# Modulation vectors of a diffusion trunk: thirteen as row sums from one ordered list, three as products

## The chip, the cores and the metric

The kernel runs on one core of one Trainium2 chip. The metric is the device time of one execution in microseconds (us). The engines in the rows are PE (TensorE, matmuls; PEld is its weight load), DVE (VectorE), ACT (ScalarE), POOL (GpSimd) and SP (SyncE, which issues the weight loads). Each works through its own instructions in order and waits on semaphores for the others.

## What is computed

Two layers run over 128 context tokens and 128 latent tokens with the same weights. What matters here is the modulation: for each layer nine vectors of 1024, for two conditions (the context's learned vector and the latent's), enter the norms as shift and scale and the residuals as gate.

```python
def adaln(cvec, w, b):
    m = jax.nn.silu(cvec) @ w + b
    return jnp.split(m, N_MOD, axis=-1)

def trunk_layer(x, mods, lp, lam_init, ctx):
    sh1, sc1, gt1, sh2, sc2, gt2, sh3, sc3, gt3 = mods
    g = lp['g_norm']
    u = modulate(rms_norm(x, g[0]), sh1, sc1)
    x = x + 0.5 * gt1[:, None, :] * swiglu(u, lp['w_ffn1_in'], lp['w_ffn1_out'])
    u = modulate(rms_norm(x, g[1]), sh2, sc2)
    y, ctx_out = token_mixer(u, lp, lam_init, ctx)
    x = x + gt2[:, None, :] * y
    u = modulate(rms_norm(x, g[2]), sh3, sc3)
    x = x + 0.5 * gt3[:, None, :] * swiglu(u, lp['w_ffn2_in'], lp['w_ffn2_out'])
    return x, ctx_out
```

The mixer computes one projection W_in of u (z), three branches from it (differential attention, a Fourier mix, a bidirectional mLSTM), their merge with sigmoid gates, and W_out.

## The kernel before

The residual `xT` stays on chip, channels on partitions, in eight blocks of 128 x 256 (128 context and 128 latent columns). Every large product is computed in two parts for precision: a weight unit of up to 128 x 1024 is split into `whi` (ScalarE, L1484) and `wlo` (VectorE, L1485), and `mm3` issues three matmuls per block (L166 to L168). A unit of eight blocks is thus 24 matmuls of TensorE.

The program is a list of steps that `add` builds and the loop at the end runs through once, in Python, so the list's order is the order of the instructions on each engine. A step needs its units; after its own function the loop calls `pump_split`, which splits coming units while fewer than six (`N_SPLIT`) are live, and then the functions in `late`. Weights come in chunks of mostly 1 MB through six buffers (`N_RAW`), loaded by SP in the order of their first need; a chunk's buffer is given to the next one when its last unit is used.

A layer has an FFN (gate and value part of eleven pairs, four units each; output part of 24 units), the mixer (W_in, then for each of three branches its gates and its product, merged into `mg`, then the output projection of eight blocks) and a second FFN. The branches' own work runs in `lanes`, generators advanced by the mixer's steps. `residual` adds a block with its gate to `xT` and puts the next norm's work on that block into `late`: square and sum (ScalarE, GpSimd), the scaled block `y` and its two parts `yh`, `yl`. The last two blocks' part is `held` and done inside `first`, the step that starts the next part: it computes products on the unnormalised `y` while `stats`, `root` (`var`, then `rstd` on GpSimd), `diag` (`dg`) and `spread` (a broadcast by TensorE) make the norm's factor, and `apply` then writes the normalised `uh`, `ul`. The last steps ahead of `first` are marked so that they pump no splits.

A modulation vector is made in one of two ways. A product (`side` in `mod_steps`) multiplies the raw weights with both conditions on TensorE in four column groups, in two steps of eight matmuls, each two passes; a closing step transposes the sums, and `finish` adds the bias. A row sum reads the transposed weights `w_adaT`, 128 rows of 1024 to an instruction, multiplies them by a condition that lies on all partitions (`cb`) and accumulates, on VectorE: 16 such steps and a `finish` give a vector. Vectors 0 and 1 of layer 0 are made in `begin`. Of the other sixteen, `ADA` lists seven as row sums and nine as products, each in a part of the program, and `spread_into` puts the steps of a part at equal distances into it.

Of the kernel before, what the change touches and what calls it, by code (L numbers as in the profile page):

```python
# [119 lines left out]


@with_exitstack
def trunk_kernel(ctx: ExitStack, tc: tile.TileContext, a: dict):
# [94 lines left out]
    run = {"lanes": False}  # L218
# [77 lines left out]

    def mod_steps(mods_):
# [20 lines left out]
        def finish(l, m, o, x):  # L318
            bT = parT[l][:, m * KD:(m + 1) * KD].unsqueeze(2).to_broadcast([P, KD, 2])
            ve.tensor_add(o, x, bT)  # L320
            if m % 3 == 1:
                k0 = 72 + m // 3 * KD
                gT = parT[l][:, k0:k0 + KD].unsqueeze(2).to_broadcast([P, KD, 2])
                ve.scalar_tensor_tensor(o, o, 1.0, gT, op0=ALU.add, op1=ALU.mult)
            elif m % 3 == 2 and m != 5:
                ve.tensor_scalar(o, o, 0.5, None, op0=ALU.mult)

        for i, (l, m) in enumerate(on_ve):
            o, junk = mods[l, m], []
            for j in range(KD // 2):  # L330
                ch = Chunk(a["w_adaT"][l, m, j], 2, D)
                for b in range(2):
                    for g in range(2):
                        u = Unit(ch, b, b + 1, 0, D, split=False)

                        def fn(u=u, k=2 * j + b, g=g, o=o, l=l, m=m, junk=junk):
                            if not junk:
                                junk.append(blk([P, D], "junkw"))
# [1215 lines left out]
```

## Time and profile before

| | |
|---|---|
| median of 3 runs (lowest, highest) | 1361.5 us (1358.19, 1361.8) |
| profiled execution, its own time | 1359.85 us |
| its span, first to last instruction | 1358.1 us |
| mean granted TensorE clock | 0.99 of full |
| busy: PE, DVE, ACT, POOL | 98%, 71%, 50%, 8% of the span |
| read from HBM | 298.85 MB |

A busy row counts the time in which an engine has at least one instruction running; matmuls overlap, so busy tells nothing of how well each is used. Times in the rows are from the span's start. In a row of the timeline the first number is the start, the second the length, and a bracket at the end gives the idle time just before it and who ended that.

### The profile page before, as it was taken

Reading aid. Unit: us, or ns where it says so; the run is one execution under the profiler, and the core shown is the slowest. Engines: PE = TensorE matmul, PEld = TensorE weight load, DVE = VectorE, ACT = ScalarE, POOL = GpSimd, SP = SyncE. Lnnn points to the kernel's source line nnn. Section 1 sums busy time; section 2 is a strip of 40 time slices with the busy share of each in tenths; the row PEclk is TensorE's granted clock in tenths of the full one; section 3 lists DMA queues with packets and bytes.
Section 4 is the critical chain, followed back from the end, with each engine's and each line's share of the span. In section 5 each row is a group of like instructions: output and inputs, shape, how many; then the busy total and the mean of one; then the engine's idle time right before and its main releaser. Section 6 shows DMA issues by size and latency. Waiting matters only on the chain.

```text
span 1358.1 us, 25895 instructions
## 1 busy us (share of the span) xinstructions
PE 1328.9 (98%) x10752; PEld 1258.0 (93%) x10752; DVE 959.8 (71%) x1533; ACT 683.0 (50%) x1096; POOL 113.4 (8%) x137
## 2 busy tenths in 40 slices
PE   6999999999999999999999999999999999999998
PEld 3899999888998998999999999988899899999998
DVE  4589865786557589977669977677565668886653
ACT  4554444665544465444455444456554445744442
POOL 3000001300000030000020000130000001200001
PEclk8999999999999999999999999999999999999999
DMA  9999966563578846987538987648445895477630
GB/s 301 325 318 324 309 213 192 173 201 125 170 250 295 266 152 215 337 306 235 181 124 296 303 304 229 203 132 232 134 155 194 292 307 186 145 259 228 223 108 32
DMA packets 239990, 304.73 MB, mean 224 GB/s; under 512 B 5552, under 2 KB 212672, under 8 KB 236160
## 3 DMA queue, kind: packets, MB, share of 16 engines
q1 hardware_dynamic: 238048, 296.98, 66.8%
q0 software_dynamic: 1824, 6.10, 1.3%
q8 instruction: 84, 1.38, 0.4%
q14 instruction: 34, 0.28, 0.1%
HBM read 298.85 MB, written 3.15 MB: 222 GB/s over the span
## 4 chain that ended last, share of the span: by engine, by line
PE 84%; DVE 8%; DMA 3%; ACT 2%; issue 1%; SPq 0%; POOL 0%; DVEq 0%; ACTq 0%
PE pm L166 25%; PE pm L167 24%; PE pm L168 24%; PE pd L163 3%; DVE wlo L1485 3%; PE pb L163 2%; DMA raw<-w_ada 2%; DVE v L488 2%; ACT whi L1484 1%; DVE ul L178 1%; PE pm L742 1%; PE pm L743 1%; PE pm L744 1%; PE pa L163 1%; DVE junkw L339 1%
## 5 line engine op out<-in xcount | busy, mean ns | idle before, releaser
L1485 DVE TENSOR_TENSOR wlo<-raw,whi 128x1024 fp32r<-128x1024 f32 (+1 forms) x424 | 507.8, 1204 | 271.2 <-ACT whi L1484 263.6
L1484 ACT CAST whi<-raw 128x1024 fp32r<-128x1024 f32 (+1 forms) x424 | 433.5, 1032 | 337.2 <-PE pm L167 247.1
L166 PE MATMUL pm<-uh,whi 128*128 128x256 f32 x1928 | 551.3, 286 | 0.0
L168 PE MATMUL pm<-uh,wlo 128*128 128x256 f32 x1928 | 541.9, 281 | 4.8 <-DVE wlo L1485 4.8
L167 PE MATMUL pm<-ul,whi 128*128 128x256 f32 x1928 | 544.5, 282 | 1.7 <-DVE v L488 1.2
L166 PEld LDWEIGHTS pm<-uh,whi 128*128 128x128 f32 x1928 | 364.4, 189 | 15.8 <-ACT whi L1484 7.7
L168 PEld LDWEIGHTS pm<-uh,wlo 128*128 128x128 f32 x1928 | 364.3, 189 | 6.1 <-DVE wlo L1485 6.1
L167 PEld LDWEIGHTS pm<-ul,whi 128*128 128x128 f32 x1928 | 364.0, 189 | 3.8 <-DVE v L488 1.7
L167 PE MATMUL pm<-hl,whi 128*128 128x256 f32 x704 | 198.0, 281 | 0.0
L166 PE MATMUL pm<-hh,whi 128*128 128x256 f32 x704 | 197.6, 281 | 0.0
L168 PE MATMUL pm<-hh,wlo 128*128 128x256 f32 x704 | 197.5, 280 | 0.0
L339 DVE CUSTOM_DVE_ANT_0 junkw<-raw,cb 128x1024 f32<-128x1024 f32 x112 | 136.5, 1219 | 0.1
L168 PEld LDWEIGHTS pm<-hh,wlo 128*128 128x128 f32 x704 | 132.7, 189 | 0.0
L166 PEld LDWEIGHTS pm<-hh,whi 128*128 128x128 f32 x704 | 132.7, 189 | 0.0
L167 PEld LDWEIGHTS pm<-hl,whi 128*128 128x128 f32 x704 | 132.7, 188 | 0.0
L413 POOL TENSOR_TENSOR nsum<-nsum,nsq 128x256 f32<-128x256 f32 x36 | 36.5, 1013 | 814.8 <-ACT nsq L411 814.8
L163 PE MATMUL pd<-raw,cT 128*32 128x512 f32 (+1 forms) x416 | 46.0, 559 | 11.4 <-DMA raw<-w_ada 9.6
L643 ACT ACTIVATE silu<-pm 128x512 f32<-128x512 f32 x39 | 23.3, 596 | 55.0 <-PE pm L168 55.0
L177 ACT CAST hh<-silu 128x512 fp32r<-128x512 f32 (+1 forms) x42 | 25.5, 609 | 32.7 <-DVE silu L645 32.7
L558 DVE SCALAR_TENSOR_TENSOR xT<-pm,mod,xT 128x128 f32<-128x128 f32 x96 | 28.8, 342 | 18.1 <-PE pm L168 18.0
L1228 ACT ACTIVATE sig<-pm 128x512 f32<-128x512 f32 x24 | 14.3, 598 | 50.2 <-PE pm L168 50.1
L742 PE MATMUL pm<-whi,uh 128*128 128x512 f32 x96 | 39.3, 409 | 0.0
(339 smaller groups left out, 1726.1 us busy)
## 6 DMA issues: line engine op xcount, KB each, us to landing
raw<-w_ffn_in SPq DMA_DIRECT2D x88, 1024.0 KB, 6.9
raw<-w_ada SPq DMA_DIRECT2D x36, 1024.0 KB, 5.2
raw<-w_ffn_out SPq DMA_DIRECT2D x32, 1024.0 KB, 5.6
raw<-w_in SPq DMA_DIRECT2D x32, 1024.0 KB, 5.8
raw<-w_adaT SPq DMA_DIRECT2D x28, 1024.0 KB, 6.7
raw<-w_branch_gate SPq DMA_DIRECT2D x24, 1024.0 KB, 5.2
raw<-w_ffn_out SPq DMA_DIRECT2D x16, 768.0 KB, 4.6
raw<-w_ada SPq DMA_DIRECT2D x16, 512.0 KB, 7.1
```

The costliest lines, as they stand in the source:

```text
L163: pe.matmul(out, lhsT, rhs, start=start, stop=stop)
L166: pe.matmul(out, sh, mh, start=start, stop=False)
L167: pe.matmul(out, sh, ml, start=False, stop=False)
L168: pe.matmul(out, sl, mh, start=False, stop=stop)
L177: ac.copy(hi, src)
L339: ve.tensor_tensor_reduce(junk[0], u.raw()[:, 0, :], cb[:, g, :], 1.0, 0.0, op0=ALU.mult, op1=ALU.add, accum_out=o[:, k, g:g + 1])
L413: eng.tensor_add(self.sum, self.sum, sq)
L488: ve.tensor_scalar(v[:, G[1]], v[:, G[1]], self.scale[:, k, 1:2], self.shift[:, k, 1:2], op0=ALU.mult, op1=ALU.add)
L558: ve.scalar_tensor_tensor(xT[:, k, G[g]], ps[:, G[g]], gate[:, k, g:g + 1], xT[:, k, G[g]], op0=ALU.mult, op1=ALU.add)
L742: pe.matmul(ps[g], xh[:, G[g]], wh, start=(k == 0), stop=False)
L1484: ac.copy(u.hi, r)
L1485: ve.tensor_sub(u.lo, r, u.hi.bitcast(F32))
```

## The change

`ADA` keeps three products: layer 0's vector 2 in its first FFN, and vector 5 of each mixer. The other thirteen stand in `ROWS`, in the order in which they are made; `row_steps` yields their 208 steps. Every step of the program carries a rate: 0.85 in the gate and value part of an FFN, 0.7 in its output part, 0.3 in W_in and the first two branches, 0.9 from the third branch on to the mixer's end; zero in the start of the program. When the sum of the rates passes one, the next row step is put behind that step. The list lasts from layer 0's first FFN to the third branch of layer 1. `finish` moves out of `mod_steps` unchanged, the target of the products that a row sum throws away becomes one fixed bf16 tile, `residual` asserts that its vectors are made, and `s_params2` (lambdas, masks) moves up by two pairs.

```diff
-CT = 8
-
-ADA = {(0, "ffn1"): ([(0, 4), (0, 3)], [(0, 2)]),
-       (0, "mixer"): ([], [(0, 7), (0, 6), (0, 5)]),
-       (0, "ffn2"): ([(1, 1), (1, 0)], [(0, 8)]),
-       (1, "ffn1"): ([(1, 4), (1, 3)], [(1, 2)]),
-       (1, "mixer"): ([], [(1, 7), (1, 6), (1, 5)]),
-       (1, "ffn2"): ([(1, 8)], [])}
+CT = 0
+
+ADA = {(0, "ffn1"): [(0, 2)], (0, "mixer"): [(0, 5)], (1, "mixer"): [(1, 5)]}
+ROWS = [(0, 4), (0, 3), (0, 7), (0, 6), (1, 1), (1, 0), (0, 8), (1, 2), (1, 4), (1, 3), (1, 7), (1, 6), (1, 8)]
+
+RATE = {"in": 0.85, "out": 0.7, "win": 0.3, "branch": 0.3, "merge": 0.9}
...
+    junkw = const.tile([P, D], BF16, name="junkw")
...
     def add(fn, units=(), pump=True, ln=False, ahead=()):
         steps.append(Step(fn, units, pump, ln, ahead))
+        steps[-1].rate = run["rate"]
...
+    def row_steps():
+
+        for l, m in ROWS:
+            o = mods[l, m]
+            for j in range(KD // 2):
+                ch = Chunk(a["w_adaT"][l, m, j], 2, D)
+                for b in range(2):
+                    for g in range(2):
+                        u = Unit(ch, b, b + 1, 0, D, split=False)
+
+                        def fn(u=u, k=2 * j + b, g=g, o=o, l=l, m=m):
+                            ve.tensor_tensor_reduce(junkw, u.raw()[:, 0, :], cb[:, g, :], 1.0, 0.0,
+                                                    op0=ALU.mult, op1=ALU.add, accum_out=o[:, k, g:g + 1])
+                            if k == KD - 1 and g == 1:
+                                finish(l, m, o, o)
+                                known.add((l, m))
+
+                        yield fn, [u]
...
+        run["rate"] = 0.0 if begun else RATE["in"]
         for jj in range(n_pair):
-            if jj == 4 and l == 0 and which == 1:
+            if jj == 2 and l == 0 and which == 1:
                 add(s_params2)
+                run["rate"] = RATE["in"]
...
         p1 = len(steps)
+        run["rate"] = RATE["out"]
...
+        run["rate"] = RATE["win"]
         add(lambda: first(norm, us, q_done), us, pump=2)
...
         p0 = len(steps) + 6
+        run["rate"] = RATE["branch"]
...
+                    if bi == 2:
+                        run["rate"] = RATE["merge"]
                     add(drain)
...
+    todo, due = row_steps(), 0.0
+    for s in steps:
+        s.slot = []
+        due += s.rate
+        while due >= 1.0:
+            due -= 1.0
+            nxt = next(todo, None)
+            if nxt is not None:
+                s.slot.append(Step(*nxt))
+    steps[:] = [x for s in steps for x in (s, *s.slot)]
+    assert next(todo, None) is None
```

A row step is an ordinary step, so it also pumps splits. The order of instructions shows what this makes of three places.

First, TensorE where layer 0's mixer comes to the branch of the attention. `uh`, `ul` are the normalised input that the gates use, `ah` the attention's output; `raw` with `cT` is a product. Before:

```order
L166 MATMUL pm<-uh_2787,whi 128x256
L167 MATMUL pm<-ul_2789,whi 128x256
L168 MATMUL pm<-uh_2787,wlo 128x256
L163 MATMUL pd<-raw_4358,cT 32x512 x4
L163 MATMUL pd<-raw_4437,cT 32x512 x4
L166 MATMUL pm<-ah,whi 128x256
```

After:

```order
L165 MATMUL pm<-uh_2813,whi 128x256
L166 MATMUL pm<-ul_2815,whi 128x256
L167 MATMUL pm<-uh_2813,wlo 128x256
L165 MATMUL pm<-ah,whi 128x256
L166 MATMUL pm<-al,whi 128x256
```

The product's matmuls between the gates and the branch are gone; in the whole program 6 such pieces remain of 18.

Second, VectorE at the end of layer 0's merge. `sig` is a branch's product times its gate, `mg` the merged sum and `mgl` its second part, `xT` the residual's update by the first two blocks of the output projection. Before:

```order
L1256 TENSOR_TENSOR sig<-sig,pm 128x512
L1257 TENSOR_TENSOR mg_4390<-mg_4390,sig 128x512
L178 TENSOR_TENSOR mgl_5319<-mg_4390,mgh_5318 128x512
L1256 TENSOR_TENSOR sig<-sig,pm 128x512
L1257 TENSOR_TENSOR mg_4390<-mg_4390,sig 128x512
L178 TENSOR_TENSOR mgl_5319<-mg_4390,mgh_5318 128x512
L1485 TENSOR_TENSOR wlo<-raw_5070,whi 128x1024 x2
L558 SCALAR_TENSOR_TENSOR xT<-pm,mod_5_101,xT 128x128 x4
```

After (the two rows with `junkw` and without are one row sum):

```order
L1267 TENSOR_TENSOR sig<-sig,pm 128x512
L1268 TENSOR_TENSOR mg_4417<-mg_4417,sig 128x512
L177 TENSOR_TENSOR mgl_5327<-mg_4417,mgh_5326 128x512
L319 ISA junkw,mod_1_106<-raw_4955,cb 128x1024
L319 ISA mod_1_106 128x1
L1509 TENSOR_TENSOR wlo<-raw_5087,whi 128x1024
L1267 TENSOR_TENSOR sig<-sig,pm 128x512
L1268 TENSOR_TENSOR mg_4417<-mg_4417,sig 128x512
L177 TENSOR_TENSOR mgl_5327<-mg_4417,mgh_5326 128x512
L1509 TENSOR_TENSOR wlo<-raw_5087,whi 128x1024
L319 ISA junkw,mod_1_106<-raw_5167,cb 128x1024
L319 ISA mod_1_106 128x1
```

A row sum and a split now stand between the last two blocks of the merge, and the second split and another row sum ahead of `xT`.

Third, VectorE at the end of the same output projection, where the second FFN's norm begins with `var`. Before:

```order
L558 SCALAR_TENSOR_TENSOR xT<-pm,mod_5_101,xT 128x128 x2
L1485 TENSOR_TENSOR wlo<-raw_5151,whi 128x1024
L426 TENSOR_SCALAR y<-xT,mod_7_103 128x128
L178 TENSOR_TENSOR yl_5431<-y,yh_5429 128x256
L558 SCALAR_TENSOR_TENSOR xT<-pm,mod_5_101,xT 128x128 x4
L463 TENSOR_SCALAR var<-pb 128x2
```

After:

```order
L559 SCALAR_TENSOR_TENSOR xT<-pm,mod_5_101,xT 128x128 x2
L1509 TENSOR_TENSOR wlo<-raw_5297,whi 128x1024
L426 TENSOR_SCALAR y<-xT,mod_7_103 128x128
L177 TENSOR_TENSOR yl_5443<-y,yh_5441 128x256
L559 SCALAR_TENSOR_TENSOR xT<-pm,mod_5_101,xT 128x128 x2
L319 ISA junkw,mod_1_106<-raw_5332,cb 128x1024
L319 ISA mod_1_106 128x1
L1509 TENSOR_TENSOR wlo<-raw_5371,whi 128x1024
L559 SCALAR_TENSOR_TENSOR xT<-pm,mod_5_101,xT 128x128 x2
L319 ISA junkw,mod_1_106<-raw_5332,cb 128x1024
L319 ISA mod_1_106 128x1
L1509 TENSOR_TENSOR wlo<-raw_5371,whi 128x1024
```

`var` comes next there: behind each of the last two blocks stand a row sum and a split. The same pattern stands at the end of both first FFNs, and at the end of layer 0's second FFN one row sum with two splits.

## Rows read from the trace of the kernel before

**Rows 1.** The page, busy us (share of the span) xinstructions of each engine:

```profile
PE 1328.9 (98%) x10752; PEld 1258.0 (93%) x10752; DVE 959.8 (71%) x1533; ACT 683.0 (50%) x1096; POOL 113.4 (8%) x137
```

**Rows 2.** Busy time by stretch: stretch, us, busy by engine, clock, DMA share, GB/s:

```profile
0.00:55.00 55.00, 41.09 (x308) 27.99 (x309) 22.66 (x56) 21.01 (x40) 11.81 (x20) 0.84 1.05 305
55.00:1340.00 1285.00, 1274.92 (x10346) 1217.70 (x10345) 933.78 (x1469) 659.82 (x1053) 100.15 (x115) 1.00 0.68 223
1340.00:1358.00 18.00, 12.94 (x103) 12.35 (x101) 3.41 (x9) 2.21 (x4) 1.48 (x2) 0.84 0.16 59
```

**Rows 3.** Chain that ended last, pieces of products: start, us, what:

```profile
382.63 1.85 PE pd L163 x16
...
1083.46 1.85 PE pd L163 x16
```

**Rows 4.** Timeline of PE, transposes of a closing step:

```profile
1122.07 0.60 PE L171 MATMUL pd<-cst,adaev 128*128 128x128 f32 x4
```

**Rows 5.** PE's waits for a product's weights, 500 to 560 and 720 to 760 us:

```profile
PE pd L163 <- DMA raw<-w_ada: 0.8, 1, 0.8
...
PE pd L163 <- DMA raw<-w_ada: 0.7, 1, 0.7
```

**Rows 6.** Timeline of DVE in layer 0's first FFN, a row sum and a split:

```profile
105.76 1.22 DVE L339 CUSTOM_DVE_ANT_0 junkw<-raw,cb 128x1024 f32<-128x1024 f32 x1
...
106.91 1.22 DVE L1485 TENSOR_TENSOR wlo<-raw,whi 128x1024 fp32r<-128x1024 f32 x1
```

**Rows 7.** That FFN's gate and value part by stretch; DVE's timeline in its output part:

```profile
100.00:165.00 65.00, 65.00 (x550) 63.43 (x549) 60.20 (x84) 30.17 (x36) 0.00 (x0) 1.00 0.96 330
...
176.83 1.23 DVE L1485 TENSOR_TENSOR wlo<-raw,whi 128x1024 fp32r<-128x1024 f32 x1 [1.61 <-ACT whi L1484]
179.67 1.23 DVE L1485 TENSOR_TENSOR wlo<-raw,whi 128x1024 fp32r<-128x1024 f32 x1 [1.61 <-ACT whi L1484]
```

**Rows 8.** Busy time by stretch, end of layer 0's mixer:

```profile
476.00:500.00 24.00, 24.00 (x205) 24.00 (x205) 21.73 (x43) 14.77 (x28) 6.87 (x6) 1.00 0.52 177
```

**Rows 9.** Timeline of DVE in layer 0's output projection:

```profile
492.66 0.59 DVE L558 SCALAR_TENSOR_TENSOR xT<-pm,mod,xT 128x128 f32<-128x128 f32 x2
...
494.31 0.76 DVE L426 TENSOR_SCALAR y<-xT,mod 128x128 f32<-128x128 f32 x1
...
495.33 0.60 DVE L558 SCALAR_TENSOR_TENSOR xT<-pm,mod,xT 128x128 f32<-128x128 f32 x2
```

**Rows 10.** End of layer 0's merge: timeline of PE and of DVE:

```profile
476.05 0.28 PE L166 MATMUL pm<-mgh,whi 128*128 128x256 f32 x1
...
478.35 0.69 DVE L178 TENSOR_TENSOR mgl<-mg,mgh 128x512 fp32r<-128x512 f32 x1 [0.69 <-ACT mgh L177]
```

**Rows 11.** Timeline of DVE, last update and the norm's start:

```profile
498.91 0.61 DVE L558 SCALAR_TENSOR_TENSOR xT<-pm,mod,xT 128x128 f32<-128x128 f32 x2 [0.32 <-PE pm L168]
501.13 0.16 DVE L463 TENSOR_SCALAR var<-pb 128x2 f32<-128x2 f32 x1 [1.62 <-PE pb L163]
501.21 0.28 DVE L426 TENSOR_SCALAR y<-xT,mod 128x128 f32<-128x128 f32 x1
```

**Rows 12.** Timeline of DVE, from layer 0's first FFN to the mixer:

```profile
232.51 0.61 DVE L558 SCALAR_TENSOR_TENSOR xT<-pm,mod,xT 128x128 f32<-128x128 f32 x2 [1.52 <-PE pm L168]
234.74 0.16 DVE L463 TENSOR_SCALAR var<-pb 128x2 f32<-128x2 f32 x1 [1.61 <-PE pb L163]
```

**Rows 13.** PE's waits in the attention, 286 to 296 and 946 to 956 us:

```profile
PE pa L171 <- DVE pc L855: 1.1, 1, 1.1
...
PE pa L171 <- DVE pc L855: 1.4, 1, 1.4
```

**Rows 14.** Busy time by stretch, clock after a stall:

```profile
34.00:36.00 2.00, 1.65 (x16) 0.68 (x16) 0.13 (x1) 0.00 (x0) 0.00 (x0) 0.50 0.91 239
...
952.00:954.00 2.00, 2.00 (x15) 2.00 (x14) 1.63 (x4) 1.96 (x6) 1.08 (x2) 0.69 0.05 6
```

**Rows 15.** Busy time by stretch, most of layer 0's branches:

```profile
340.00:470.00 130.00, 130.00 (x1091) 119.51 (x1090) 79.11 (x132) 59.90 (x101) 4.64 (x5) 1.00 0.74 249
```

More of the change, by code (lines that the diff above doesn't have):

```diff
@@ L119, in __init__ @@
         self.ahead = list(ahead)
+        self.rate = 0.0
 @with_exitstack
@@ L217, in trunk_kernel @@
     lanes = [[], [], []]
-    run = {"lanes": False}
+    run = {"lanes": False, "rate": 0.0}
     late, held = [], []
@@ L316, in side @@
                 ac.copy(st["ev"], st["ps"])
[L318 to L338, printed above, removed]
-                            ve.tensor_tensor_reduce(junk[0], u.raw()[:, 0, :], cb[:, g, :], 1.0, 0.0,
-                                                    op0=ALU.mult, op1=ALU.add, accum_out=o[:, k, g:g + 1])
-                            if k == KD - 1 and g == 1:
-                                finish(l, m, o, o)
-                        seq.append(((i + (4 * j + 2 * b + g) / 16) / len(on_ve), fn, [u]))
         for i, (l, m) in enumerate(mods_):
@@ L356, in fn @@
                               for e in range(2) for c in range(2)], 0, 512)
-                seq.append(((2 * i + j2 + 0.4) / (2 * len(mods_)), fn, us))
-        seq.sort(key=lambda x: x[0])
-        out = [x[1:] for x in seq]
-        if not mods_:
-            return out
+                out.append((fn, us))
         def post():
@@ L378, in post @@
                 finish(l, m, mods[l, m], full[:, :, 2 * i:2 * i + 2])
+                known.add((l, m))
         out.append((post, []))
@@ L554, in prod8, with residual @@
                 mid()
-    def residual(k, ps, gate, norm):
+    def residual(k, ps, gate, norm, of):
+        assert of <= known, (of, known)
         for g in range(2):
@@ L585, in add_ffn @@
         gate = mods[l, 2 if which == 1 else 8]
+        of = {(l, 2), (l, 3), (l, 4)} if which == 1 else {(l, 8), (l + 1, 0), (l + 1, 1)}
+        of = {x for x in of if x[0] < DEPTH}
         hT = {}
@@ L1268, in mk_ @@
             return mg["h", k // 4][:, k % 4, :], mg["l", k // 4][:, k % 4, :]
-        gate = mods[l, 5]
+        gate, of = mods[l, 5], {(l, 5), (l, 6), (l, 7)}
         for mp in range(4):
@@ L1288, in fn @@
                     prod8(p_, u, mk_)
-                    residual(m, p_, gate, norm_next)
+                    residual(m, p_, gate, norm_next, of)
                 add(fn, [us_[i]], pump=mp < 3)
-        spread_into(p0, len(steps) - 8, mods_)
+        if mods_:
+            spread_into(p0, len(steps) - 8, mods_)
         return loads
@@ L1414, in trunk_kernel @@
     for l in range(DEPTH):
-        add_ffn(l, 1, norms[l, 0], norms[l, 1], ADA[l, "ffn1"], begin if l == 0 else None)
+        add_ffn(l, 1, norms[l, 0], norms[l, 1], ADA.get((l, "ffn1")), begin if l == 0 else None)
         pos = len(steps)
-        steps.insert(pos - 6, Step(add_mixer(l, norms[l, 1], norms[l, 2], ADA[l, "mixer"]), pump=False))
-        add_ffn(l, 2, norms[l, 2], norms[l + 1, 0], ADA[l, "ffn2"])
+        steps.insert(pos - 6, Step(add_mixer(l, norms[l, 1], norms[l, 2], ADA.get((l, "mixer"))), pump=False))
+        add_ffn(l, 2, norms[l, 2], norms[l + 1, 0], ADA.get((l, "ffn2")))
     def fin():
```

20 lines of the change are left out of this document (15 added, 5 removed).

## The prediction

> **What bounds the kernel now.** I read the busy line first. TensorE is busy 98% of the span, VectorE 71% [rows 1]. Then where TensorE is idle: of 29.1 us, 19.0 lie in the first 55 us and the last 18 us, which the change leaves nearly as they are, and 10.1 are spread over the 1285 us between [rows 2]. So a microsecond of TensorE work taken out of the middle is a microsecond gained, as long as VectorE, which takes the work over, keeps up everywhere. Its share is an average, and I look for stages in which it has no room. The sum is made against the profiled execution, 1359.85 us around a span of 1358.1; it lies 1.65 us under the median of the three runs, 1361.5, within their spread of 3.6.
>
> **Products removed.** A modulation product is two pieces of 16 TensorE passes, and a piece holds the in-order TensorE for 1.85 us [rows 3], which show the first and the last of those that go; of 18 pieces 12 go, four in each mixer and two each in layer 0's second FFN and layer 1's first. 12 x 1.85 = 22.2 us. Of five closing steps two go, each with four transposes, 0.60 us [rows 4]: 1.2 us. In those two FFNs a product also waited for its weights, 0.8 and 0.7 us [rows 5]: 1.5 us, gone with it. Gain: 24.9 us, all on the path that sets the end.
>
> **Rows added.** 208 row sums stand in place of 112, so 96 more. In a full queue one takes VectorE 1.14 us (from the row at 105.76 to the split at 106.91, the accumulator read hidden) [rows 6]: 110 us. Most of it is hidden. With a row at nearly every step layer 0's first FFN ran VectorE at 93% while TensorE was busy throughout [rows 7], so the rate of 0.85 in the other gate and value parts, about what two of them have now, costs nothing. In the output parts a split comes every 2.84 us, takes 1.23 and leaves 1.61 idle before the next [rows 7]: a row at 0.7 a step fits. Layer 1's second FFN loses its rows. The DMA volume does not change. The bf16 target of the row I cost at nothing; it is written by the same stream. The lambda steps, two pairs earlier in layer 0's first FFN, bring their two table loads and small operations with them; they stay under the splits done ahead.
>
> **Where it does not fit: the end of layer 0's mixer.** In the output projection VectorE repeats update, split, two scalings in one group and difference in 2.67 us (from xT at 492.66 to xT at 495.33) [rows 9], and TensorE's step is 2.84: no room. From 476 to 500 us VectorE is busy 21.7 of 24 us [rows 8]. The new order puts seven row sums between the last merge block but one and the last xT, and one split ahead of it that used to come after: 8 x 1.14 = 9.1 us. Of the 2.3 us idle some 0.5 can take a row; the rest are waits inside a chain (sig, mg, the ScalarE cast, mgl) that remain. So the last xT ends 8.6 us later. Behind it one row and one split (2.3 us) stand ahead of var, where 1.62 us were idle [rows 11]: 0.7 more. var starts the norm's chain, for which TensorE waits at its next broadcast, and PSUM buffers that xT frees are late too, so TensorE cannot run ahead. **9.2 us.** Bounds: 10 instructions x 1.14 less all idle time, 11.4 - 3.9 = 7.5, to 11.4.
>
> **Three other norms.** Row steps now stand between the last block of an FFN and the next norm, where no step pumped splits before, and each also lets a split go ahead. For both mixers two rows and two splits come ahead of var (4.6 us) where 1.5 and 1.6 us were idle [rows 12]; with the wait for ScalarE's cast I get var 2.0 us later. Some 0.7 comes back, as those splits are not to be done after the norm: 1.3 each. From layer 0 to layer 1 it is one row and two splits, 3.4 less 1.6, of which 0.4 comes back: 1.4. Sum **4.0 us**, bounds 0 and 7.
>
> **Layer 1's merge.** One row and one split stand ahead of the last sig, and VectorE comes there 0.5 to 1 us late: the last mgl, ready at 478.35 + 0.69 in layer 0's copy of the place, comes 2.8 us later. TensorE starts on mgh at 476.05 [rows 10] and needs the last block after 36 matmuls of 0.12 us, at 480.4, so 1.3 us are slack: **1.5 us** (0 to 2.8). In layer 0 the same wait is inside the 9.2.
>
> **Attention in the mixers.** TensorE waits 1.1 and 1.4 us for pc [rows 13]. At 0.3 rows a step one or two rows fall into the full stretch ahead of it: 1.5 + 1.1 = **2.6 us** (0 to 5, four rows, since earlier ones fall into VectorE's wait for the swapped queries). Nothing of SP's queue is new there but row chunks in place of weight columns; the swap is issued behind a load that waits for a split on VectorE, as now.
>
> **Clock.** At 950 to 954 us a stall of 1.4 us is followed by a granted clock of 0.69 of 2.4 GHz, and after the wait for weights near the start the clock was 0.50, its 1.2 GHz level, for 34 to 36 us [rows 14]. Longer stalls now stand at five places: I take **2 us** (0 to 6). The Trainium skill (TensorE: Matmul & The Clock Gate, part 1, The HAM clock gate) calls the half rate the default and activity what releases it; the rows agree, and by it each stall is paid again in slow matmuls, the second rival.
>
> **A rule against the rows.** Where VectorE's scaling y runs beside GpSimd's sums in the output projection it takes 0.76 us, and 0.28 when alone [rows 9, 11]. The Trainium skill (SBUF — State Buffer, Summary: rules for kernel authors) says that a VectorE instruction with two SBUF inputs and a GpSimd one that reads SBUF block each other; a row has two. By the trace the collision is already in the 2.67; by the rule rows could collide as well, six sums by 0.48 or 2.9 us, which the range holds.
>
> **Sum.** 24.9 - (9.2 + 4.0 + 1.5 + 2.6 + 2.0) = 24.9 - 19.3 = 5.6 us gained: 1359.85 - 5.6 = **1354 us**.
>
> **Rivals.**
> *VectorE catches up.* The idle time inside the chains takes rows after all, and the stalls overlap: losses at their lower bounds or slightly above, 8 to 10 us. For it: layer 0's first FFN ran at 93% without a stall. Against it: the 2.67 of 2.84 us. 1359.85 - 24.9 + 9 = 1344 us.
>
> *Slower by the clock.* One mechanism at the end of layer 0's mixer and behind the four other stalls: TensorE is starved, falls to 1.2 GHz and runs half-fast when its work is there again. Near the start 34 to 38 us were run so, 2 us lost. It decides when the clock costs over 11.7 us in place of 2 (24.9 + 4.1 - 17.3), that is 2 us at each place and some 4 at the mixer's end; with the other losses near their upper bounds the time is 1359.85 - 24.9 + 31 = 1366 us. Against it: the dip at 952 us is 0.31 of 2 us, some 1.2 us at the half rate, and cost 0.6 us.
>
> *The gain is eaten.* If the output projection costs its upper bound and each norm the full 2 us that var is late, losses are some 25 us: 1360 us, no change. For it: nothing may come back after the norms. Against it: two splits less behind each.
>
> *The products go, but not their time.* That would need TensorE to wait where the product stood, for lanes that the product covered. In layer 0's merge it is busy in all 130 us [rows 15], while it also waits for the lanes' results there, and VectorE has a third of that time free; at most the 7.4 us of one layer's products would be lost, which ends at 1361 and in the case above.
>
> **How the numbers follow.** Forecast (1348 to 1357) 0.52; VectorE catches up (1340 to 1348) 0.20; eaten (1357 to 1364) 0.20; slower by the clock (over 1364) 0.08. A measurement can tell 0.3% (4.1 us) from no change, that is 1357.4 and 1365.6 around the median. Faster: 0.52 + 0.20 = 0.72, less a little for the forecast's edge and the offset between profiled time and median: 0.70. Same 0.22, slower 0.08. The range leaves out half of the first rival and the slow one: 1344 to 1364.
>
> **What the profile after would show.** 12 pieces of products fewer, 6 left. VectorE's busy time up by some 110 us. At the end of layer 0's mixer the last xT some 9 us behind TensorE's last matmul, TensorE with gaps of several us before the broadcast, perhaps a clock of 0.5 there. var 2 us later after its xT at the next norms. Layer 1's second FFN unchanged. I am wrong if TensorE's idle time between the ends stays near 10 us (then 1340), or if VectorE's queue makes TensorE wait inside an FFN's gate and value part, which I hold to be free.

## The result

The changed kernel takes 1370.4 us (median of 4 runs, 1370.0 to 1373.1) beside 1361.2 us for the kernel before (median of 4): a ratio of 1.0076, with a 95% interval of 1.0056 to 1.0096. It is slower by 9 us. Forecast were 1354 us, faster, and a range of 1344 to 1364. The traces compared below stand further apart than the medians, 13.2 us, since the profiled execution of the changed kernel is the slowest of its four.

The page of the changed kernel, the busy line and the group of row sums (group: count, busy us, mean ns, idle before):

```profile
PE 1320.1 (96%) x10551; PEld 1268.0 (92%) x10552; DVE 1069.2 (78%) x1719; ACT 683.4 (50%) x1094; POOL 112.6 (8%) x137
...
L319 DVE CUSTOM_DVE_ANT_0 junkw<-raw,cb 128x1024 bf16<-128x1024 f32 x208 | 253.9, 1221 | 0.0
```

Against [rows 1] VectorE is busy 109.4 us more, as the sum had it, and a row sum still takes 1.22 us. TensorE is busy 8.8 us less. The work that was taken out is 12 x 1.85 + 1.2 = 23.4 us, so 14.6 us of TensorE's busy time came back: the same matmuls ran longer. And the span is 13.2 us longer, so TensorE's idle time (span less busy) went from 29.2 to 51.2 us, 22.0 more. Busy time by stretch, as in [rows 2], says where:

```profile
0.00:55.00 55.00, 40.23 (x298) 28.35 (x300) 22.38 (x55) 20.29 (x38) 11.75 (x20) 0.88 1.05 304
55.00:1353.00 1298.00, 1266.82 (x10158) 1227.22 (x10157) 1043.40 (x1656) 660.87 (x1053) 99.37 (x115) 0.98 0.67 221
1353.00:1371.00 18.00, 13.02 (x99) 12.41 (x98) 3.41 (x9) 2.21 (x4) 1.49 (x2) 0.81 0.16 60
```

The two ends are nearly as they were. In the middle TensorE is idle 31.2 us, before 10.1. Its waits there, from 60 to 1350 us (engine, line, what it waited for: us in total, times, longest):

```profile
PE pm L749 <- ACT v L759: 8.4, 2, 5.4
PE pm L165 <- ACT mgh L176: 5.0, 2, 3.1
PE pb L162 <- ACT dg L470: 4.1, 3, 2.1
PE pb L162 <- ACT nsq L411: 3.8, 3, 1.7
PE pm L165 <- DVE xT L559: 3.3, 3, 2.0
PE pa L170 <- DVE pc L862: 3.3, 2, 2.9
```

In the first row v is the attention's value block; mgh is the merged branches; dg and nsq belong to the norm; xT is the residual's update, pc the attention's weights. The largest wait, for v, was not in the prediction at all. Busy time by stretch behind those waits; the granted clock is the third number from the end:

```profile
300.00:310.00 10.00, 10.00 (x73) 9.89 (x72) 7.19 (x12) 5.63 (x12) 1.08 (x2) 0.86 0.40 115
484.00:488.00 4.00, 3.88 (x21) 3.88 (x22) 3.75 (x9) 2.63 (x5) 0.00 (x0) 0.61 0.36 105
508.00:518.00 10.00, 8.56 (x38) 8.32 (x39) 7.81 (x18) 6.44 (x13) 2.33 (x3) 0.51 0.58 211
709.00:713.00 4.00, 4.00 (x23) 4.00 (x23) 3.96 (x7) 2.55 (x8) 3.64 (x5) 0.58 0.61 211
900.00:907.00 7.00, 6.42 (x30) 5.94 (x29) 5.39 (x12) 4.13 (x13) 3.56 (x5) 0.51 0.47 150
948.00:955.00 7.00, 5.18 (x13) 4.08 (x14) 5.01 (x9) 4.24 (x6) 0.76 (x1) 0.52 0.75 216
1150.00:1157.00 7.00, 6.85 (x35) 6.69 (x35) 5.96 (x13) 3.79 (x7) 1.59 (x1) 0.56 0.52 170
```

The clock has two levels, 1.2 and 2.4 GHz, so a mean of 0.51 over 10 us is 9.8 us at 1.2 GHz. Summed so, the seven rows hold 39 us at the lower level. The kernel before had one such place in the middle, behind the wait at 950 us [rows 14]; it went on behind the row shown there:

```profile
954.00:956.00 2.00, 2.00 (x11) 2.00 (x11) 1.73 (x3) 1.76 (x3) 0.00 (x0) 0.50 0.56 171
```

That makes 1.2 us up to 954 and 2.0 behind it, over 3 us at the lower level.

**Where it went.** The same matmul can be found in both traces, and the difference of its start times tells how far the changed kernel is ahead or behind there. The table gives how that difference grows from one such matmul to the next (us; times of the kernel before), and the same for three of the kernels that follow: all rows narrow, all rows narrow without splits behind them, and all rows placed, the second time. Differences of up to 0.2 us depend on which matmul is taken as a boundary.

| from, to | what lies there | changed | narrow rows | narrow, no splits | placed, second |
|---|---|---|---|---|---|
| 0, 141 | start | +1.1 | +0.3 | 0.0 | +0.6 |
| 141, 255 | FFN 1 to mixer, layer 0 | +1.3 | +1.2 | +2.0 | +3.1 |
| 255, 294 | input projection, attention | +6.4 | +2.6 | +0.3 | -0.6 |
| 294, 462 | branches, 4 pieces out | -7.7 | -8.3 | -8.3 | -7.8 |
| 462, 484 | third branch | +4.0 | 0.0 | -0.2 | -0.2 |
| 484, 519 | output projection, norm | +7.4 | +2.7 | +0.3 | +0.1 |
| 519, 627 | FFN 2, 2 pieces out | -5.5 | -5.5 | -5.4 | -5.4 |
| 627, 716 | layer 0 to layer 1 | +1.9 | +1.9 | -0.1 | 0.0 |
| 716, 800 | FFN 1, 2 pieces out | -4.9 | -4.9 | -4.8 | -4.9 |
| 800, 914 | FFN 1 to mixer, layer 1 | +3.1 | +2.2 | +3.8 | +3.8 |
| 914, 958 | input projection, attention | +5.1 | +2.3 | +1.5 | -2.6 |
| 958, 1122 | branches, 4 pieces out | -7.2 | -7.7 | -7.6 | -7.5 |
| 1122, 1145 | third branch | +6.9 | +0.3 | 0.0 | 0.0 |
| 1145, 1309 | rest | +0.4 | +0.4 | +0.7 | +0.4 |
| sum | | +12.4 | -12.4 | -17.8 | -20.9 |

The stretches in which products went out gain 25.3 us, where the sum said 24.9. The others lose 37.6, where it said 19.3. These losses hold both kinds, waits and slow matmuls. For the stretch from 462 to 519 the busy times are (before, then the changed kernel with the same matmuls at both ends):

```profile
462.00:519.00 57.00, 56.03 (x466) 55.40 (x465) 46.41 (x90) 34.58 (x65) 13.97 (x14) 1.00 0.43 141
463.11:531.56 68.45, 61.66 (x466) 60.46 (x466) 62.65 (x117) 35.65 (x67) 13.75 (x14) 0.90 0.52 173
```

Of the 11.4 us that it lost 5.8 are idle time (68.45 - 61.66 against 57.00 - 56.03) and 5.6 are the same 466 matmuls taking longer, at a mean clock of 0.90.

### The profile page after: what moved, and what is told of

The parts are those of the page before. It is cut to its first block, busy times and chain, and to the rows that moved or that the text cites. A ratio compares the mean times of both kernels' runs of the same rounds, so it can differ in the third digit from the quotient of the medians.

```text
span 1371.3 us, 25714 instructions
## 1 busy us (share of the span) xinstructions
PE 1320.1 (96%) x10551; PEld 1268.0 (92%) x10552; DVE 1069.2 (78%) x1719; ACT 683.4 (50%) x1094; POOL 112.6 (8%) x137
## 4 chain that ended last, share of the span: by engine, by line
PE 78%; DVE 12%; issue 3%; ACT 3%; DMA 3%; SPq 1%; POOL 1%; DVEq 0%; ACTq 0%; POOLq 0%
PE pm L165 23%; PE pm L166 23%; PE pm L167 23%; DVE wlo L1509 3%; DVE junkw L319 2%; PE pb L162 2%; PE pd L162 2%; DMA raw<-w_ada 2%; DVE v L488 1%; ACT whi L1508 1%; DMA kl<-q 1%; DVE ul L177 1%; PE pa L162 1%; DVE xT L559 1%; PE pa L170 1%
## 5 line engine op out<-in xcount | busy, mean ns | idle before, releaser
L319 DVE CUSTOM_DVE_ANT_0 junkw<-raw,cb 128x1024 bf16<-128x1024 f32 x208 | 253.9, 1221 | 0.0
L411 ACT ACTIVATE nsq<-xT 128x256 f32<-128x256 f32 x42 | 17.6, 418 | 60.4 <-DVE xT L559 60.4
L165 PE MATMUL pm<-mgh,whi 128*128 128x256 f32 x128 | 38.0, 297 | 5.5 <-ACT mgh L176 5.0
```

The costliest lines, as they stand in the source:

```text
L165: pe.matmul(out, sh, mh, start=start, stop=False)
L319: ve.tensor_tensor_reduce(junkw, u.raw()[:, 0, :], cb[:, g, :], 1.0, 0.0, op0=ALU.mult, op1=ALU.add, accum_out=o[:, k, g:g + 1])
```

## The experiments

All times are medians. The ratios, with 95% intervals, are to the kernel before as it ran beside each of them (1360.8, 1360.3 or 1359.7 us).

**Rows that cost VectorE next to nothing.** Which part of the loss is the row sums' time on VectorE? In this kernel and the next two a row sums 16 of 1024 elements, everywhere or in some parts, and leaves out the rest of the sum; order, loads and splits stay.

```
-  ve.tensor_tensor_reduce(junkw, u.raw()[:, 0, :], cb[:, g, :], ...)
+  n = 16 if run["part"] in NARROW else D
+  ve.tensor_tensor_reduce(junkw[:, 0:n], u.raw()[:, 0, 0:n], cb[:, g, 0:n], ...)
+  NARROW = ("in", "out", "win", "branch", "merge")
```

> All 208 row sums are kept in their places with their loads, but each sums 16 of its 1024 elements, so the vectors' values are left out and VectorE is some 230 us less busy. Aligned at equal steps, the changed kernel against the one before shows 12 pieces that save 24.3 us and stretches that lose 37.5 us. Theory 1 (VectorE's row time makes the losses): 1370.4 - 37.5 = 1333 us, taking 1330 to 1338. Theory 2 (the loads of the rows make part of them, since the swapped queries land 1.0 and 3.2 us later): 1338 to 1343 us. Rival (the products' time does not go): 1350 us or more.

1348.8 us, 0.9914 (0.9899 to 0.9929). The products' time does go, and the rows' time on VectorE costs 21.6 us in the changed kernel. But the time is neither the 1333 of theory 1 nor the 1338 to 1343 of theory 2, although the rows take 0.17 us each. (Theory 1 was 4 us too low by itself: it took 37.5 us, read between traces 13.2 us apart, from a median that is 9.1 away.) By the table some 14 us stay lost, most of them at the four norms (1.2, 2.7, 1.9, 2.2) and in the attention (2.6, 2.3).

**The same in the merge and the output projection alone** (NARROW = ("merge",)).

> Only the row sums at the third branch and the output projection of both layers sum 16 of 1024 elements (their values are left out). The stretch from layer 0's last branch to the norm's broadcast lost 12.7 us and layer 1's last branch 6.9 us. Theory 1 (VectorE is full there): 1370.4 - 18.5 = 1352 us, 1349 to 1356. Rival (what is gained there is lost again behind it, at the norm and in the clock): 1360 to 1366 us.

1356.6 us, 0.9977 (0.9966 to 0.9987): 13.8 us back, between the two. What does not come back is the norm behind it, 3.7 of 7.4 us.

**The same in the input projections and the first two branches alone** (NARROW = ("win", "branch")).

> Only the row sums behind the mixers' input projections and first two branches sum 16 of 1024 elements (their values are left out); all loads stay. Those stretches lost 6.4 and 5.1 us. Theory 1 (rows on VectorE ahead of the rotary step delay it): 1370.4 - 11.5 = 1359 us. Theory 2 (the swapped queries land later because of the loads that stand ahead of them in SP's queue): of the 11.5 us 4 to 8 stay, 1363 to 1367 us.

1363.2 us, 1.0018 (1.0008 to 1.0027): 7.2 us back, at the edge of theory 2. Compared as in the table, 4.2 us come back in layer 0's attention, 1.3 in layer 1's, and 3.3 at layer 1's third branch, where no row was made narrow: VectorE came there with less work behind it. The sum of the two kernels, 13.8 + 7.2 = 21.0, is near the 21.6 of all rows, but the third branch stands in both, so it is no exact division. That the rows in the FFNs cost next to nothing is read from the table: the FFN stretches gain the same with full and with narrow rows (5.5 and 4.9).

**Matmuls that fill the waits.** TensorE is given matmuls on constants at the places of the waits.

```
+  def filler(n):
+      t = pd([P, 256])
+      for _ in range(2 * n):
+          mm(t, identb, flat(maskb))
...
+  filler(4)    # ahead of norm.stats()
+  filler(5)    # ahead of norm.spread()
+  filler(10)   # ahead of the Fourier product
+  filler(8)    # first step of the output projection
+  filler(4)    # its last steps, layer 0
```

> The changed kernel with matmuls on constants (0.1 us each at the full clock, 8 to 20 at a place) put where TensorE waits: ahead of the norms' statistics and broadcasts, ahead of the Fourier product, in the output projection. They fill waits and change no result. TensorE's busy time fell by 8.8 us where 23.4 were taken out, and seven dips to 1.2 GHz of 3.4 to 10.2 us lie behind the stalls. Theory 1 (the clock costs 14.6 us): fewer dips and 1356 to 1363 us. Rival (the dips fall on time in which TensorE waits anyway, or the fillers only take the place of the waits): 1369 to 1373 us.

1371.3 us, 1.0076 (1.0059 to 1.0092): the rival's time. Two rows of its timeline, twenty and ten fillers, give 0.11 us each ((2.36 - 1.26) / 10), so the 186 are 20.5 us at the full clock. Two groups of ten ran at the lower level, one of them in the third row:

```profile
939.66 2.36 PE L162 MATMUL pd<-maskb,identb 128*128 128x256 bf16 x20
704.71 1.26 PE L162 MATMUL pd<-maskb,identb 128*128 128x256 bf16 x10
512.24 2.36 PE L162 MATMUL pd<-maskb,identb 128*128 128x256 bf16 x10
```

Its page has TensorE busy for 1329.9 us and a span of 1369.3, so it is idle for 39.4 us, 11.8 less than in the changed kernel; of the 14.6 us by which the matmuls were too long some 4 are left, the slow fillers' share among them (1329.9 - 1305.5 - 20.5 = 3.9, where 1305.5 is 1328.9 less 23.4). So fillers do give most of the clock's time back, some 10.7 us, and cost it: 20.5 us of work against 11.8 + 10.7. The slow clock is a price of the stalls, by estimate 0.4 us for each us at the lower level (14.6 for 39). Fewer fillers, or other places, were not tried.

The price does not come with every stall. In the kernel with narrow rows in the merge TensorE waits 2.1 us for dg at the norm between the layers, as in the changed kernel, and its clock there stays full:

```profile
699.00:704.00 5.00, 4.55 (x36) 4.52 (x37) 4.47 (x10) 3.81 (x11) 3.38 (x5) 1.00 0.63 213
```

The stretch from layer 0 to layer 1 loses 0.4 us in that kernel and 1.9 in the changed one, where the clock was 0.58 from 709 to 713 us. So 3.4 us at the lower level cost 1.5 there. What decides whether the clock falls behind a stall these runs do not settle.

**No splits behind rows.** A row step no longer lets weight splits go ahead.

```
-  s.slot.append(Step(*nxt))
+  s.slot.append(Step(*nxt, pump=False))
```

> The changed kernel with one difference: a row step no longer lets weight splits go ahead behind it. With all rows at a sixty-fourth of their width the norms between parts still lost 1.2, 2.7, 1.9 and 2.1 us against the kernel before. Theory 1 (the splits that a row step lets go ahead of the norm's var make that loss): 1370.4 - 7.9 = 1362.5 us, 1360 to 1365. Rival (the row sums themselves, 1.14 us each, are enough to keep var late): 1367 us or more.

1364.3 us, 1.0030 (1.0017 to 1.0042): 6.1 us back, within theory 1's 1360 to 1365. Its places are others, though. Step by step against the changed kernel, the norm from layer 0 to 1 gains 2.0, the two third branches 2.5 each, the two attentions 1.1 and 2.2, the start 1.3; the end of layer 0's mixer, its first branches and the norms ahead of the mixers lose 0.6, 0.8, 1.4 and 1.1. At the end of layer 0's mixer, where the row sums alone fill VectorE, taking the splits away gained nothing.

**Both together**: rows of 16 elements, and no splits behind them.

> All row sums over 16 of 1024 elements (values left out), and no splits behind row steps: VectorE has neither the rows' time nor the splits ahead of the norms. Theory 1: 1348.8 - 7.9 = 1341 us, 1339 to 1343, and what is then left over 1337 us is the two waits for the swapped queries (2.6 and 2.4 us). Rival (the norms' loss comes from something else, the order of the small operations): 1346 us or more.

1343.6 us, 0.9880 (0.9865 to 0.9895), 0.6 us above theory 1's bracket. The norm between the layers shows what the splits did. VectorE's timeline of the changed kernel, from the last update to var:

```profile
702.38 0.61 DVE L559 SCALAR_TENSOR_TENSOR xT<-pm,mod,xT 128x128 f32<-128x128 f32 x2 [0.41 <-PE pm L167]
702.90 1.48 DVE L319 CUSTOM_DVE_ANT_0 junkw<-raw,cb 128x1024 bf16<-128x1024 f32 x1
...
704.47 2.36 DVE L1509 TENSOR_TENSOR wlo<-raw,whi 128x1024 fp32r<-128x1024 f32 x2
706.75 0.15 DVE L463 TENSOR_SCALAR var<-pb 128x2 f32<-128x2 f32 x1
```

and of the kernel without splits, whose row still has its full length:

```profile
700.25 0.61 DVE L559 SCALAR_TENSOR_TENSOR xT<-pm,mod,xT 128x128 f32<-128x128 f32 x2 [0.41 <-PE pm L167]
700.77 1.48 DVE L319 CUSTOM_DVE_ANT_0 junkw<-raw,cb 128x1024 bf16<-128x1024 f32 x1
...
702.49 0.16 DVE L463 TENSOR_SCALAR var<-pb 128x2 f32<-128x2 f32 x1 [0.23 <-PE pb L162]
```

One row and two splits ahead of var make 4.37 us from xT to var; with the row and without the splits it is 2.24, and 2.25 in the kernel of this experiment. At this norm the two splits are the loss and the row fits: it goes from 1.9 (narrow rows, splits kept) to nothing in both kernels without splits. At the end of layer 0's mixer, where rows and splits both go, the loss goes from 2.7 to 0.3. The two norms ahead of the mixers do not gain (2.0 and 3.8), for another reason than the one that holds in the changed kernel. There TensorE waits for the norm's sums and factor (nsq 0.9 and 1.7 us, dg 1.4 and 0.6). Here these waits are gone, but in layer 1 TensorE now waits 2.8 us for the normalised v, which GpSimd holds up (below), and in layer 0 its idle time is no more than before, but the clock falls:

```profile
249.50:257.00 7.50, 7.01 (x31) 6.31 (x31) 6.63 (x16) 4.47 (x8) 0.32 (x2) 0.54 0.64 224
```

**The late swap.** In the attention VectorE waits for queries that four small DMAs on SP's queue have swapped between partitions. In the changed kernel's layer 0 VectorE waits 4.87 us for them (before: 3.91), in layer 1 7.81 (before: 4.61). Layer 1, on VectorE:

```profile
942.96 0.69 DVE L816 TENSOR_TENSOR kl<-kl,cst 128x512 f32<-128x512 f32 x1 [7.81 <-DMA kl<-q]
```

on ScalarE, behind that:

```profile
946.95 0.42 ACT L1006 ACTIVATE gpk<-gpk 40x256 f32<-40x256 f32 x1 [9.11 <-DVE gpk L1004]
...
949.19 1.06 ACT L759 COPY v<-pm 128x512 f32<-128x512 f32 x2
```

and SP's queue ahead of it (start, us from first issue to last landing):

```profile
920.42 0.34 SPq L1486 DMA_DIRECT2D raw<-w_adaT  x1
926.75 5.32 SPq L1486 DMA_DIRECT2D raw<-w_in  x3
932.16 3.59 SPq L811 DMA_DIRECT2D kl<-q  x4
```

VectorE stands for 7.8 us, gpk behind it, ScalarE's copy of v behind gpk, and TensorE, which needs the PSUM tile that v frees, for 5.4. Ahead of the swap, SP took a chunk for rows, then had no free buffer for 6 us, then three weight loads in one burst. Is it that a chunk with four rows at 0.3 a step holds one of six buffers for some 13 steps? This kernel has the rows of 16 elements of the third experiment, but the four rows of a chunk stand together:

```
-  while due >= 1.0:
-      due -= 1.0
+  while due >= (4.0 if s.part in NARROW and n % 4 == 0 else 1.0) or (s.part in NARROW and n % 4):
+      due, n = due - 1.0, n + 1
```

> As the kernel with narrow row sums behind the input projections and first two branches (1363.2 us; same values left out), but the four rows of one loaded chunk stand together there, so the chunk holds one of the six weight buffers for a moment instead of some 13 steps. In that kernel SP issues three weight loads right ahead of the swapped queries, and VectorE waits 5.6 and 9.1 us for them, 3.9 and 4.6 in the kernel before. Theory 1 (the held buffer delays the loads into the swap): waits of 4 to 5 us and 1363.2 - 4.7 = 1358.5 us. Rival (the swap is late for another reason): 1362 to 1364 us.

1366.7 us, 1.0046 (1.0031 to 1.0061), with waits of 6.07 and 7.86 us, where the kernel that it starts from had 5.60 and 9.14: theory 1 fell. The rival's 1362 to 1364 was missed as well; 28 narrow rows stand there in place of 36, so eight more rows have full length, and the third branches lose 1.3 and 2.3 us more. A chunk stood right ahead of the burst here too (at 256 and 918 us), and how long it was held made little difference to the waits. What the traces do show: in layer 1 the wait was 7.7 to 9.4 us in the eight kernels that have a chunk loaded right ahead of the swap, and 4.1 to 5.7 in the six that have none there, the kernel before among them. No kernel moved that chunk alone, so that the chunk is the cause is argued, not shown.

**All rows placed.** The same row sums and products; each part has its number of rows, in whole chunks of four.

```
-  RATE = {"in": 0.85, "out": 0.7, "win": 0.3, "branch": 0.3, "merge": 0.9}
+  QUOTA = {(0, 1, "in"): 36, (0, 1, "out"): 16, (0, "branch"): 16, (0, 2, "in"): 40, (0, 2, "out"): 16,
+           (1, 1, "in"): 36, (1, 1, "out"): 16, (1, "branch"): 16, (1, 2, "in"): 16}
...
+  for part, n in QUOTA.items():
+      at = [s for s in steps if s.part == part]
+      at = {"in": at[part[:2] != (0, 1):], "out": at[:20], "branch": at[2:]}[part[-1]]
+      for i in range(n):
+          at[i * len(at) // n].slot.append(Step(*next(todo)))
```

> The same 13 row vectors and 3 products with full sums, placed by part in whole chunks of four rows: one row a step in the FFNs' gate and value parts (36, 40, 36 and 16 rows), 16 rows in the first 20 steps of each output part but the last, 16 in the first two branches of each mixer, none in the input projection, the third branch, the mixer's output projection or just ahead of a norm. Theory 1 (only the places are wrong): 1361.2 - 24.3 = 1337 us with up to 6 us for VectorE's fuller parts, 1336 to 1343. Rival (96 more rows cost TensorE time wherever they stand): 1352 us or more.

1340.3 us, 0.9853 (0.9839 to 0.9868), within theory 1's 1336 to 1343: 96 more row sums are all but free where VectorE has room. One cost was new: 1.63 and 1.31 us of waits for ha, behind rows at the second branch.

**Rows back into the merge of layer 0** (12, taken from its second FFN and first branches), all else as placed.

```
-  (0, "branch"): 16, (0, 2, "in"): 40
+  (0, "branch"): 12, (0, "merge"): 12, (0, 2, "in"): 32
```

> The placed kernel with 12 rows in layer 0's third branch and output projection (taken from its second FFN, 8, and its first two branches, 4). Theory 1 (VectorE is full there: 2.67 of 2.84 us a step in the output projection): 12 x 1.14 = 13.7 us less some 3 to 5 idle, some 10 us late at the norm, and the clock on top: 1340.3 + 10 = 1350 us, 1348 to 1354. Rival (the loss needs what came ahead of it in the changed kernel, the splits behind the last steps): 1341 to 1345 us.

1350.3 us, 0.9932 (0.9917 to 0.9947): 10.0 us for 12 rows, as forecast. In the two stretches from 462 to 519 us 10.4 are lost, 5.9 of them idle time and 4.5 longer matmuls. Busy time between the same two times as in [rows 8], some 6 us further on in the work:

```profile
476.00:500.00 24.00, 18.68 (x151) 17.86 (x150) 23.58 (x48) 11.46 (x24) 5.66 (x5) 0.99 0.60 195
```

VectorE is busy 23.6 of 24 us (21.7 before), and TensorE 18.7 (24.0 before): one is full while the other waits for it.

**Rows back into the input projections** (8 of each mixer's 16).

```
-  (l, "branch"): 16
+  (l, "win"): 8, (l, "branch"): 8
```

> The placed kernel with 8 of the 16 rows of each mixer's branches moved into its input projection, two chunks of four rows. Theory 1 (a chunk of rows there takes one of six weight buffers out of turn, the weight loads come in a burst ahead of the swapped queries, and VectorE's queue waits): waits for the swap of 5 to 9 us in place of 4.53 and 5.04, and with the rows' own time 1340.3 + 4 to 8 = 1344 to 1348 us. Rival (the input projection holds 8 rows at no cost): 1339 to 1341 us.

1345.8 us, 0.9894 (0.9879 to 0.9909): theory 1's time, 5.5 us lost, but not its way. The chunks came to stand behind the swap (at 278 and 926 us), and it was not late:

```profile
274.15 0.69 DVE L817 TENSOR_TENSOR kl<-kl,cst 128x512 f32<-128x512 f32 x1 [3.20 <-DMA kl<-q]
...
922.11 0.69 DVE L817 TENSOR_TENSOR kl<-kl,cst 128x512 f32<-128x512 f32 x1 [4.06 <-DMA kl<-q]
```

The loss is at pc, for which TensorE waits 1.93 and 2.93 us in place of 0.56 and 0.52, and in the clock behind that. So the rows' own time there is a price of its own, without any late swap.

**Placed, a second time**: 12 and 8 rows in the branches, 20 in the output parts.

```
-  (0, 1, "out"): 16, (0, "branch"): 16, (0, 2, "out"): 16, (1, 1, "out"): 16, (1, "branch"): 16
+  (0, 1, "out"): 20, (0, "branch"): 12, (0, 2, "out"): 20, (1, 1, "out"): 20, (1, "branch"): 8
-  "out": at[:20], "branch": at[2:]
+  "out": at[:22], "branch": at[:14]
```

> The placed kernel (1340.3 us) with fewer rows in the mixers' first two branches (12 and 8 in place of 16 and 16, and within the first 14 steps) and 20 in place of 16 in the first 22 steps of the output parts. In the placed kernel TensorE waits 1.63 and 1.31 us for ha, behind rows at the second branch. Theory 1: these 2.9 us come back, 1337 to 1338 us. Rival (the output parts have no room for four more rows each, and the norms wait again): 1341 us or more.

1336.4 us, 0.9828 (0.9812 to 0.9845): 23 us (21 to 26) better than before, and faster than both kernels. TensorE's waits from 60 to 1316 us:

```profile
PE pm L167 <- DVE v L489: 5.6, 2, 2.8
PE pm L168 <- DVE wlo L1509: 3.1, 5, 0.8
...
```

The largest that is left is at the start of the mixers, the stretches with +3.1 and +3.8 in the table.

**Two clearings on VectorE.** At the start of the mixers VectorE's scaling v takes ten times its usual time while GpSimd issues three DMAs and clears five blocks.

```
-  po.memset(gh.bitcast(F32), 0.0)
-  po.memset(gl.bitcast(F32), 0.0)
+  ve.memset(gh.bitcast(F32), 0.0)
+  ve.memset(gl.bitcast(F32), 0.0)
```

> As the kernel sent with it (fewer rows in the branches), and two blocks are cleared by VectorE in place of GpSimd at the start of the mixers. In all kernels with rows VectorE's scaling v takes 4.3 us there in place of 0.34, until GpSimd has done its three DMA issues and its clearings, and 2.13 us in the kernel before, until the third issue. Theory 1 (the two engines exclude each other): v takes 2.1 to 2.6 us, TensorE waits some 2 us less in each mixer, of which VectorE's clearings take back 1: 2 us under the other kernel. Rival (the wait is on something else): v stays at 4.3 us, and the time within 1 us or above.

1333.9 us, 0.9806 (0.9790 to 0.9822): 2.6 us under the other, where 2 were forecast; the runs of the two do not overlap, by 0.6 us (1335.5 is the other's lowest, 1334.9 this one's highest). v takes at most 0.76 us, even beside the three issues, not the 2.1 to 2.6 that theory 1 wanted; so the waits go altogether, and 1.3 and 2.6 us come back as waits for the attention's v. This edit has nothing to do with the row sums, and in the two stretches this kernel is 1.7 us ahead of the one before each time. It was not tried in the kernel before.

## Why the prediction was wrong

**Right.** The gain: 24.9 forecast, 25.3 measured in the stretches with pieces, and 23 us under the kernel before with placed rows says that nearly all of it can be had. VectorE's 110 us. What the FFNs hold: a row at nearly every step cost nothing. The rival that the products go but not their time is out.

**Where the sum went wrong.** The prediction priced stalls by place and the clock by a term of its own, so the losses of the table have to be divided in the same way. TensorE's idle time and its busy time, each taken between the same matmuls in both traces, do that (us):

| place | stalls forecast | more idle time | longer matmuls | loss |
|---|---|---|---|---|
| end of layer 0's mixer | 9.2 | 5.8 | 5.6 | 11.4 |
| three other norms | 4.0 | 4.0 | 2.3 | 6.3 |
| layer 1's merge | 1.5 | 3.3 | 3.6 | 6.9 |
| attention, both layers | 2.6 | 9.1 | 2.4 | 11.5 |
| start and rest | 0 | 0.9 | 0.6 | 1.5 |
| sum | 17.3 | 23.1 | 14.5 | 37.6 |

Two terms failed: the attention's stall, 2.6 in place of 9.1, and the clock, 2.0 in place of some 14.5. The merge of layer 1 was too small as well, and the largest term, the end of layer 0's mixer, too large.

**The end of layer 0's mixer: right mechanism, too large.** 9.2 us of stalls (7.5 to 11.4) were forecast (its two parts, 8.6 and 0.7, make 9.3). The loss there is 11.4, which looks like a hit, but half of it is the clock: the stalls are 5.8, under the lower bound. That VectorE is full there is shown: twelve rows put back into an else free kernel cost 10.0, again with 5.9 of idle time. The last update ended 10.7 us late (510.78 against 498.91, less the 1.2 us by which the kernel was late ahead of it), where 8.6 had been worked out; TensorE was partly slow meanwhile, so not all of that was waiting. VectorE's timeline, as in [rows 11]:

```profile
510.78 0.60 DVE L559 SCALAR_TENSOR_TENSOR xT<-pm,mod,xT 128x128 f32<-128x128 f32 x2
...
514.00 0.15 DVE L463 TENSOR_SCALAR var<-pb 128x2 f32<-128x2 f32 x1
```

**Norms: right in sum.** Forecast were 1.3, 1.4 and 1.3 us of stalls; more idle time is 2.0, 1.1 and 0.9, and the waits there are for nsq, which follows the last update, and for dg, which follows var: rows and splits stand ahead of both. That the sums agree to 4.0 is in part luck, as no single one does. Between the layers it is the splits and not the row that make var late. The losses, 1.3, 1.9 and 3.1, hold the clock as well. Ahead of the mixers the held scaling v would have come next: TensorE waits 1.1 us for it in layer 0 of the changed kernel (0.6 before) and not at all in layer 1, but 2.8 us in both layers of the placed kernels, where it does not wait for nsq or dg.

**Layer 1's merge: mis-sized, 1.5 in place of 3.3.** "One row and one split stand ahead of the last sig" counted the instructions that had moved past it, not the queue behind which it stands. VectorE's timeline there:

```profile
1131.81 1.22 DVE L319 CUSTOM_DVE_ANT_0 junkw<-raw,cb 128x1024 bf16<-128x1024 f32 x1
...
1132.95 1.22 DVE L1509 TENSOR_TENSOR wlo<-raw,whi 128x1024 fp32r<-128x1024 f32 x1
...
1140.93 1.22 DVE L319 CUSTOM_DVE_ANT_0 junkw<-raw,cb 128x1024 bf16<-128x1024 f32 x1
...
1142.07 0.69 DVE L1267 TENSOR_TENSOR sig<-sig,pm 128x512 f32<-128x512 f32 x1
```

Five rows and four splits stand ahead of this sig without a gap, 10.3 us. ScalarE had it ready at 1136.9, and VectorE came to it 5.2 us later. The prediction did see 2.67 of 2.84 us in the output projection; here, too, there was no room. TensorE then waited at 1149.59:

```profile
1149.59 0.58 PE L165 MATMUL pm<-mgh,whi 128*128 128x256 f32 x1 [3.11 <-ACT mgh L176]
```

**Attention: wrong place, 2.6 in place of 9.1.** The step that failed is "nothing of SP's queue is new there but row chunks in place of weight columns". Rows of 0.3 a step were priced at the wait that the trace of before showed, for pc. The new wait stood ahead of it: swapped queries that land later, VectorE in order behind them, ScalarE behind VectorE, v behind ScalarE. In layer 0 most of the loss is the rows' own time (4.2 of 6.4 us come back when the rows are narrow there); in layer 1 most is not (1.3 of 5.1), and there VectorE waits 3.2 us longer for the swap than before. Why the swapped queries land later stays open.

**The clock: 2 in place of some 15 us.** This is the largest miss, and the prediction's own rival had the case: slower by the clock, 1366 us, with a chance of 0.08, "when the clock costs over 11.7 us". It cost 14.6. What failed is the price of one fall. The prediction read the dip of [rows 14] in the two us from 952 to 954, took it for 1.2 us at the half rate and 0.6 us of cost, and came to 2 us for five places. The next row, shown above, has 0.50 from 954 to 956: the dip held over 3 us. And in the changed kernel the clock stays low for 6 to 10 us in four of the seven places, the longest where three waits follow each other (508 to 518 us). The Trainium skill (TensorE: Matmul & The Clock Gate, Part 1, The HAM clock gate) makes activity the condition for the full rate. The seven rows agree in part: each of the seven stretches at the lower level, 39 us in all, begins at a wait or right behind one, but not each wait has one behind it (2.1 us for dg, above, with a clock of 1.00).

By kind the miss reads: stalls 17.3 forecast, 23.5 measured (idle time 22.0 higher, and 1.5 of old waits gone; 0.4 of it lies outside the places of the table); clock 2.0 forecast, 14.6 measured. 24.9 - 23.5 - 14.6 = -13.2 us, the difference of the two spans. With the clock as forecast the two spans would have come out within 1 us of each other.

## What to carry to other kernels

An engine that is busy 78% on average is full in some parts; work given to it costs nothing in one part and 0.8 us apiece in another, so place it by part, from the busy share of each part, and do not spread it by rate over a chain that ends in a norm or a merge. Where instructions move into an in-order queue, count the whole queue ahead of the instruction that somebody waits for; a wait for a DMA in that queue holds up every engine that needs something from behind it. When stalls are added to TensorE where it is otherwise always busy, price the slow clock behind them with the stalls: here 14.6 us beside 23.5. And when a total agrees with the forecast, divide it as the forecast was divided before calling it right.

## What the runs showed of the hardware

**VectorE held off by GpSimd.** GpSimd's timeline in the changed kernel's layer 1, and below it VectorE's:

```profile
909.91 0.83 POOL L692 DMA_DIRECT2D ckv<-cache_k  x1
910.74 0.75 POOL L693 DMA_DIRECT2D ckv<-cache_v  x1
911.48 0.90 POOL L695 DMA_DIRECT2D C<-state_C  x1
912.36 0.81 POOL L697 MEMSET zgh<- 128x832 f32 x1
...
914.33 0.23 POOL L1003 MEMSET g<- 36x128 f32 x1
```

```profile
910.18 4.47 DVE L488 TENSOR_SCALAR v<-v,mod,mod 128x128 f32<-128x128 f32 x1
...
915.52 0.34 DVE L488 TENSOR_SCALAR v<-v,mod,mod 128x128 f32<-128x128 f32 x1
```

The same scaling takes 4.47 us beside GpSimd and 0.34 after it; it ends when the last clearing does. In the kernel before it took 2.13 and 2.15 us and ended with the third issue; in the kernel with narrow rows and no splits behind them 2.19 us in layer 0 and 4.32 in layer 1; with two of the clearings moved away at most 0.76. The Trainium skill (SBUF — State Buffer, Who interferes with whom) says that VectorE in one of its modes with two ports, which a tensor_scalar can enter, and GpSimd lock each other out of a shared port pair for a whole instruction, whichever starts first. The trace agrees that VectorE is held up beside GpSimd; which mode it was in, it does not show. But here it was held over eight GpSimd instructions in a row, or over three, and why it came to be the one or the other is open.

**A row sum on VectorE** of 128 x 1024 elements takes 1.22 us and one of 128 x 16 elements 0.17 us.
